# Another order at the passage from the weights' batches to the expert loop, two casts on POOL, and a place of weights read in six parts

## The chip, the cores and the metric

One NeuronCore of a Trainium2 chip runs the kernel. The metric is the device time of one execution in microseconds (us); the time before is the median of 3 runs. The profile is of one further execution.

Engines in the text: TensorE (PE; PEld is its weight load), VectorE (DVE), ScalarE (ACT), GpSimd (POOL) and SyncE (SP). SP issues most DMAs and ScalarE and POOL some. Each engine works through its own queue in order.

## The reference

One layer of a diffusion backbone over 512 tokens of width 1024: a mixer (pooling and retention, not touched here), then a feed-forward block of single-neuron experts with product keys, and a final RMSNorm. The part that matters:

```python
s = einsum('thpd,hpkd->thpk', q, keys)             # 8 heads, 2 halves, 128 keys each
s1, i1 = top_k(s[:, :, 0], 16); s2, i2 = top_k(s[:, :, 1], 16)
cand = s1[..., :, None] + s2[..., None, :]         # 16 x 16 candidates
cidx = i1[..., :, None] * 128 + i2[..., None, :]
best, pos = top_k(cand, 16); eidx = take_along_axis(cidx, pos)
g = softmax(best)
act = gelu(einsum('thkd,td->thk', u[eidx], hb))
out = einsum('thk,thkd->td', g * act, v[eidx])     # 16384 experts, u and v of width 1024
```

Each token uses 8 x 16 = 128 of the 16384 experts.

## The kernel before, in words

**Two ways to the same sum.** The 512 tokens are four blocks of 128. For block 0 the kernel gathers: for each of the 128 slots an indirect DMA on POOL's queue fetches, for each token, the row of u and v that its index names (`fetch`, L979); VectorE makes the dot product and adds the weighted row to `acc` (`dot`, `combine`, L987 and L998). For the three other blocks (384 tokens, side by side) it computes densely: the 16384 experts are taken as 128 planes of 128 experts. For a plane j, `up` multiplies its u (1024 x 128) with the tokens and applies GELU (ScalarE, L1106) into a tile `a`; the result is multiplied with a dense table G of weights, nearly all of it zeros (VectorE, L1141, "product" in the text), and `down` multiplies it with the plane's v and adds up in six PSUM banks Y.

**Three products for one.** A float32 matmul is made of three: each operand is split into `hi` (a cast, L163 for planes, L145 for `ph`) and `lo` (the difference, L168 for planes, L146 for `pl`), and `mm3` (L151 to L153) multiplies hi hi, then the two mixed ones. An `up` has 24 matmuls of 384 columns, done in two halves that a generator (`ups`, advanced by `run_up`) hands out; a `down` has 18 of 512 columns. `hi` of a plane is ScalarE's, `lo` VectorE's or POOL's.

**Loads.** Planes of u or v are 512 KB each and go by SP's queue into three buffers `raw` (L158); a load waits until `lo` has freed its buffer. `hi` and `lo` of planes have four buffers each.

**Weights.** The table G is built before the loop in 24 batches of 16 tokens (`onehots`, `weights`): one-hot matmuls into PSUM, a copy by ScalarE, a write to `gd` in HBM on ScalarE's DMA queue. The loop reads it back by places: a place has 8 planes for all tokens (1536 KB in rows of 512 bytes, as `gd` is laid out by batches), and there are 16 places and two buffers G. `place(p)` takes the buffer, `read(p, b0, b1)` issues a DMA for the batches b0 to b1 on SP's queue (L1120).

**The passage.** During the batches TensorE also runs the first `up` blocks ahead of the loop: AHEAD = 30 of them, 51 halves of 60 by the end of the batches. So 25 are complete then, number 25 is half done, and its successor 26 is split already. The order of all this part and of the loop is written out by hand (`manual_schedule`): each engine runs its instructions in program order. After the batches come, in this order: loads of v0 and v1; the last two reads of place 0; `place(1)` and its read; five times a half `up` and a `tick`; all remaining `up`s; the split of v0 (`lo` on POOL); three products; `weigh(0)`, which makes `ph` and `pl` of plane 0. `prep(n)` splits plane n of u and asks for the loads up to n + 3; within the generator it runs as the `up` before n begins.

**Ticks.** Top-k of block 0 is done head by head in five steps, each a stage of a generator (`topk`): step 1 on VectorE finds 16 of 128 in both halves, and two casts of the indices into `sf` follow (L927, L928, on ScalarE); step 2 adds up candidates on POOL (L936); step 3 on VectorE finds 16 of them; step 4 multiplies on POOL (L958); step 5 reduces on VectorE into `eidx`. `tick` (L1160) takes one new head and advances all that are under way by one step, oldest first; eight heads take 12 ticks.

**The loop.** Round j (0 to 127): read of a place in each round 8p + 6 (place p + 2), `weigh(j + 1)`, the split of v (`run_v`, up to plane j + 1; `lo` on POOL in the first 8 rounds), loads of u, `hi` of u, `down(j)`, the dot products and sums of the gathered slots with the products up to plane j + 3 between them, `lo` of u, an `up` in about four rounds of five, a `tick`. The gather begins in round GATHER = 8, with 1.2 slots a round; its buffers take the memory of block 0's top-k. In round 117 (LATE) three of its buffers are taken over for the end.

Of the kernel before, what the change touches and what calls it, by code (L numbers as in the profile page):

```python
# [20 lines left out]
P = 128  # L21
# [13 lines left out]
MG = 8  # L35
# [4 lines left out]
AHEAD = 30  # L40
JE = 121
LATE = 117
GATHER = 8
LAG = 2
CREDIT = 1.2
NT = 16
# [88 lines left out]
class Build:  # L135
# [765 lines left out]
    def topk(self, tp, h, s, blocks, bufs, eng=None):  # L901


        nc = self.nc
        NEG = -3.0e38
        n = len(blocks)
        b0 = blocks[0]
        tag = f"{n}"

        def new(shape, dt, name):  # L910
            return tp.tile([P, n] + shape, dt, name=name + tag, tag=name + tag, bufs=bufs)

        def best(of):

            for lo in (0, 8):
                for v, i, a in of:
                    nc.vector.max(out=v[:, lo:lo + 8], in_=a)
                for v, i, a in of:
                    nc.vector.max_index(i[:, lo:lo + 8], v[:, lo:lo + 8], a)
                if lo == 0:  # L920
                    for v, i, a in of:
                        nc.vector.match_replace(a, v[:, 0:8], a, NEG)

        sv, si = new([2, 16], F32, "sv"), new([2, 16], U32, "si")
        best([(sv[:, b, f], si[:, b, f], s[:, b, f]) for b in range(n) for f in range(2)])
        sf = new([2, 16], F32, "sf")
        nc.scalar.mul(sf[:, :, 0], si[:, :, 0], 128.0)  # L927
        nc.scalar.copy(sf[:, :, 1], si[:, :, 1])  # L928
        yield
        cs, ci = new([NCAND], F32, "cs"), new([NCAND], F32, "ci")  # L930
        for src, dst in ((sv, cs), (sf, ci)):
            o = 0
            for a0, m, w in CAND:
                A = src[:, :, 0, a0:a0 + m].unsqueeze(3).to_broadcast([P, n, m, w])
                B = src[:, :, 1, 0:w].unsqueeze(2).to_broadcast([P, n, m, w])
                nc.gpsimd.tensor_tensor(dst[:, :, o:o + m * w].rearrange("p h (a b) -> p h a b", a=m), A, B, ALU.add)  # L936
                o += m * w
            if b0:
                yield
        if not b0:  # L940
            yield
        bv, bi = new([16], F32, "bv"), new([16], U32, "bi")
        best([(bv[:, b], bi[:, b], cs[:, b]) for b in range(n)])

        pos = new([16, NI], F16, "pos")
        nc.vector.tensor_copy(pos, bi.unsqueeze(3).to_broadcast([P, n, 16, NI]))
        oh = tp.tile([P, n * 16, NC], F16, name="oh", tag="oh", bufs=1)
        sh = [P, n * 16, NC // NI, NI]
        nc.vector.tensor_tensor(oh.rearrange("p k (m i) -> p k m i", i=NI),
                                self.ioh[:, 0:NC].rearrange("p (m i) -> p m i", i=NI).unsqueeze(1).to_broadcast(sh),  # L950
                                pos.rearrange("p n k i -> p (n k) i").unsqueeze(2).to_broadcast(sh), ALU.is_equal)
        sl = slice(h * TOPK, (h + 1) * TOPK)
        nc.vector.tensor_tensor((self.gw if b0 else self.gw0)[:, :, sl], bv, bv[:, :, 0:1].to_broadcast([P, n, 16]), ALU.subtract)
        yield
        oe = tp.tile([P, n, 16, NCAND], F32, name="oe", tag="oe", bufs=1) if not b0 else \
            self.rt.tile([P, 2 * NB * P * NI], F32, name="oe", tag="ig", bufs=1)[:, :n * 16 * NCAND].rearrange(
                "p (n k c) -> p n k c", n=n, k=16)
        (nc.gpsimd if eng is None else eng).tensor_tensor(  # L958
            oe, oh.rearrange("p (n k) c -> p n k c", n=n)[:, :, :, :NCAND],
            ci.unsqueeze(2).to_broadcast([P, n, 16, NCAND]), ALU.mult)  # L960
        yield
        e = self.ef[:, :, sl] if b0 else new([16], F32, "e")
        nc.vector.tensor_reduce(e, oe, axis=AX.X, op=ALU.add)
        if not b0:
            nc.vector.tensor_copy(self.eidx[:, sl], e[:, 0])
# [143 lines left out]
    def experts(self):  # L1109
# [9 lines left out]
        def read(p, b0=0, b1=N // NT):  # L1119
            nc.sync.dma_start(Gs[p][:, b0:b1], self.gd[:, b0:b1, p * MG:(p + 1) * MG])  # L1120
# [4 lines left out]
        def run_v(to, eng):  # L1125

            while nv[0] < to:
                for n in range(nv[1], min(nv[0] + 2, P)):
                    vs[n] = load_v(n)
                    nv[1] += 1  # L1130
                vs[nv[0]] = self.split_w(vs[nv[0]], eng)
                nv[0] += 1
# [4 lines left out]
        def run_times(to):  # L1137
            while nt[0] < min(to, P):
                j = nt[0]
                a = acts[j].rearrange("p (b t) -> p b t", t=NT)  # L1140
                nc.vector.tensor_tensor(a, a, Gs[j // MG][:, :, j % MG], ALU.mult)  # L1141
                nt[0] += 1
# [17 lines left out]
        def tick(new=True):  # L1160

            if new:
                live.extend(islice(heads, 1))
            live[:] = [x for x in live if next(x, True) is None]
# [3 lines left out]
        with tc.tile_pool(name="hot", bufs=1) as hp:  # L1168
# [3 lines left out]
            for i, t0 in enumerate(todo):  # L1172
# [4 lines left out]
                if i in (13, 20):  # L1177
                    read(0, *{13: (0, 10), 20: (10, 18)}[i])
        self.rt_es.close()
        for n in range(2):  # L1180
            vs[n] = load_v(n)
        nv[1] = 2
        read(0, 18, 22)
        read(0, 22)
        self.dp = dp = self.pool("dense")
        place(1)
        read(1)
        for _ in range(5):
            self.run_up(1)
            tick()  # L1190
        self.run_up(2 * AHEAD)
        run_v(1, nc.gpsimd)
        self.pes.close()
        self.pp = es.enter_context(tc.tile_pool(name="pd", bufs=1, space=PSUM))
        self.ptags = {"ps": 2}
# [7 lines left out]

            return min(P, AHEAD + (j + 1) * (P - AHEAD) // JE)

        acts.update(enumerate(self.acts))
        run_times(3)
        ps[0] = weigh(0, nc.vector)

        f0 = None  # L1210

        for j in range(P):
            if j == GATHER:
                self.early.close()
                self.gp = es.enter_context(tc.tile_pool(name="gather", bufs=1, side="right"))
                self.acc = self.gp.tile([P, D], F32, name="acc", bufs=1)
            if j % MG == MG - 2 and j // MG + 2 < P // MG:
                place(j // MG + 2)
                read(j // MG + 2)
            deep = j >= JE  # L1220
            if j + 1 < P:
                ps[j + 1] = weigh(j + 1, nc.vector)
            run_v(min(P, j + 4 if deep else j + 2), nc.gpsimd if j < GATHER else nc.vector)
            while nl < goal(j + 2):
                us[nl] = self.load_u(nl)
                nl += 1
            hi = {}
            for n in range(ns, goal(j + 1)):
                hi[n] = self.split_hi(us[n])
            if j < P - 2:  # L1230
                for b in range(NB):
                    down(j, b, ps[j], vs[j])
                del ps[j], vs[j]

            ready = list(range(done, asked[0]))
            cr = [self.dot(s, slots[s]) for s in ready]
            run_times(j + 4)
            for s, act in zip(ready, cr):
                self.combine(s, slots.pop(s), act)
            done = asked[0]  # L1240
            for n in hi:
                us[n] = self.split_lo(us[n], hi[n], nc.vector)
                ns += 1
            while nu < goal(j):
                acts[nu] = self.up(nu, us.pop(nu))
                nu += 1
            tick()
            if j == GATHER - 1:
                self.softmax(self.gw0, self.z0)
            if j >= GATHER:  # L1250
                credit += CREDIT
                while credit >= 1 and fetched < S:
                    slots[fetched] = self.fetch(fetched)
                    fetched += 1
                    credit -= 1
            asked = asked[1:] + [fetched]
            if j == LATE:
                assert fetched == S
                fin = [self.gp.tile([P, 2 * D], F32, name="uv", tag="uv", bufs=NUV) for _ in range(3)]
                fin = [x[:, i * D:(i + 1) * D] for x in fin for i in range(2)]  # L1260
                self.row_bcast(fin[0], self.modc[:, 24:32])
                nc.sync.dma_start(fin[1], I["fg"].to_broadcast([P, D]))
            if LATE < j <= LATE + 4:
                b = j - LATE - 1
                nc.sync.dma_start(fin[2 + b], self.xd[b * P:(b + 1) * P])
            if j > LATE + 4 and done == S:
                if f0 is None:
                    f0 = self.finish(0, self.acc, [self.acc[:, 0:512], self.acc[:, 512:]], fin[2], fin[0], fin[1])
                    next(f0)
# [23 lines left out]
```

## Time and profile before

| | us |
|---|---|
| median of 3 runs | 1838.06 |
| the 3 runs | 1836.46, 1838.06, 1847.68 |
| the profiled execution | 1851.27 |
| its span, first to last instruction | 1849.3 |
| TensorE busy | 1751.0 (95%) |
| VectorE busy | 1346.7 (73%) |
| ScalarE busy | 776.6 (42%) |
| POOL busy | 435.6 (24%) |
| mean granted TensorE clock | 0.98 |

Times in rows are us from the start of the span. A row of the timeline has start, length, engine, line, operation, tiles, and in brackets how long the engine had been idle and what ended it. In rows of groups "x8" counts instructions. The granted clock is a share of 2.4 GHz; at 0.5 it is 1.2 GHz.

### The profile page before, as it was taken

Reading aid. Unit: us, or ns where it says so; the run is one execution under the profiler, and the core shown is the slowest. Engines: PE = TensorE matmul, PEld = TensorE weight load, DVE = VectorE, ACT = ScalarE, POOL = GpSimd, SP = SyncE. Lnnn points to the kernel's source line nnn. Section 1 sums busy time; section 2 is a strip of 40 time slices with the busy share of each in tenths; the row PEclk is TensorE's granted clock in tenths of the full one; section 3 lists DMA queues with packets and bytes.
Section 4 is the critical chain, followed back from the end, with each engine's and each line's share of the span. In section 5 each row is a group of like instructions: output and inputs, shape, how many; then the busy total and the mean of one; then the engine's idle time right before and its main releaser. Section 6 shows DMA issues by size and latency. Waiting matters only on the chain.

```text
span 1849.3 us, 25951 instructions
## 1 busy us (share of the span) xinstructions
PE 1751.0 (95%) x9913; PEld 1566.5 (85%) x9913; DVE 1346.7 (73%) x2402; ACT 776.6 (42%) x1320; POOL 435.6 (24%) x387
## 2 busy tenths in 40 slices
PE   7999999999999988877999999999999999999996
PEld 4889988888989988876898889999978898888885
DVE  6865365663569999987767688787768787767756
ACT  6343344223334358852434344443434443434333
POOL 2222220001148710024522222222212222222100
PEclk9999999999999999998999999999999999999998
DMA  7211134774142227772497798898878888887752
GB/s 304 103 47 46 58 131 131 237 243 145 63 142 92 81 101 263 277 237 89 156 374 290 274 329 309 327 331 295 328 282 303 317 308 298 333 302 266 267 170 91
DMA packets 132428, 404.00 MB, mean 218 GB/s; under 512 B 9680, under 2 KB 59088, under 8 KB 112720
## 3 DMA queue, kind: packets, MB, share of 16 engines
q1 hardware_dynamic: 109984, 241.38, 38.8%
q0 software_dynamic: 18432, 134.23, 18.4%
q10 hardware_dynamic: 3888, 26.74, 3.5%
q8 instruction: 77, 1.26, 0.3%
q14 instruction: 47, 0.39, 0.1%
HBM read 372.95 MB, written 29.36 MB: 218 GB/s over the span
## 4 chain that ended last, share of the span: by engine, by line
PE 38%; DVE 9%; DMA 8%; ACT 4%; issue 3%; POOL 1%; ACTq 0%; DVEq 0%; POOLq 0%
DMA raw<-uvd 8%; PE Y L152 7%; PE Y L153 7%; PE Y L151 7%; PE ps L153 6%; PE ps L151 6%; PE ps L152 6%; DVE lo L168 2%; DVE o L1071 2%; ACT st L1084 2%; ACT hi L163 2%; DVE eq L1068 1%; DVE uv L987 1%; DMA gd<-st 1%; DVE o L1069 0%
## 5 line engine op out<-in xcount | busy, mean ns | idle before, releaser
L168 DVE TENSOR_TENSOR lo<-raw,hi 128x1024 fp32r<-128x1024 f32 x285 | 358.6, 1259 | 139.8 <-ACT hi L163 138.4
L163 ACT CAST hi<-raw 128x1024 fp32r<-128x1024 f32 x332 | 344.0, 1050 | 267.8 <-DMA raw<-uvd 186.3
L153 PE MATMUL ps<-hfT,lo 128*128 128x384 f32 x1120 | 380.4, 340 | 17.8 <-DVE lo L168 17.8
L151 PE MATMUL ps<-hfT,hi 128*128 128x384 f32 x1120 | 382.1, 341 | 11.1 <-ACT hi L163 11.1
L152 PE MATMUL ps<-hfT,hi 128*128 128x384 f32 x1120 | 378.3, 338 | 0.1
L979 POOL DMA_INDIRECT uv<-uv,eidx x128 | 196.5, 1535 | 623.7 <-DVE acc L998 599.2
L151 PE MATMUL Y<-hi,ph 128*128 128x512 f32 x768 | 305.4, 398 | 16.5 <-ACT hi L163 12.8
L152 PE MATMUL Y<-lo,ph 128*128 128x512 f32 x768 | 307.6, 401 | 9.6 <-POOL lo L168 7.0
L153 PE MATMUL Y<-hi,pl 128*128 128x512 f32 x768 | 306.5, 399 | 0.5 <-DVE pl L146 0.5
L153 PEld LDWEIGHTS ps<-hfT,lo 128*128 128x128 f32 x1120 | 212.4, 190 | 23.9 <-DVE lo L168 23.8
L151 PEld LDWEIGHTS ps<-hfT,hi 128*128 128x128 f32 x1120 | 212.8, 190 | 16.5 <-ACT hi L163 12.3
L152 PEld LDWEIGHTS ps<-hfT,hi 128*128 128x128 f32 x1120 | 212.8, 190 | 4.4 <-POOL hfT L146 0.5
L151 PEld LDWEIGHTS Y<-hi,ph 128*128 128x128 f32 x768 | 147.7, 192 | 48.1 <-ACT hi L163 14.7
L998 DVE SCALAR_TENSOR_TENSOR acc<-uv,act,acc 128x1024 f32<-128x1024 f32 x127 | 163.1, 1284 | 33.1 <-ACT act L990 22.3
L152 PEld LDWEIGHTS Y<-lo,ph 128*128 128x128 f32 x768 | 147.4, 192 | 42.9 <-POOL lo L168 8.9
L153 PEld LDWEIGHTS Y<-hi,pl 128*128 128x128 f32 x768 | 147.6, 192 | 32.5 <-DVE pl L146 1.4
L168 POOL TENSOR_TENSOR lo<-raw,hi 128x1024 fp32r<-128x1024 f32 x47 | 117.8, 2515 | 204.5 <-ACT hi L163 204.5
L146 DVE TENSOR_TENSOR pl<-a,ph 128x384 fp32r<-128x384 f32 x128 | 75.0, 586 | 118.5 <-ACT ph L145 118.5
L1106 ACT ACTIVATE a<-ps 128x384 f32<-128x384 f32 x128 | 62.7, 490 | 227.7 <-PE ps L153 221.3
L987 DVE SCALAR_TENSOR_TENSOR uv<-uv,hf 128x1024 f32<-128x1024 f32 x128 | 154.5, 1220 | 0.0
L1084 ACT ACTIVATE st<-ps 128x512 f32<-128x512 f32 x96 | 90.9, 1111 | 13.4 <-DMA gd<-st 7.2
L989 ACT ACTIVATE act<-act 128x1 f32<-128x1 f32 x128 | 25.9, 202 | 162.4 <-DVE uv L987 162.2
(285 smaller groups left out, 2913.5 us busy)
## 6 DMA issues: line engine op xcount, KB each, us to landing
raw<-uvd SPq DMA_DIRECT2D x252, 512.0 KB, 5.8
ada<-ada SPq DMA_DIRECT2D x48, 512.0 KB, 4.9
gd<-st ACTq DMA_DIRECT2D x24, 1024.0 KB, 5.4
G<-gd SPq DMA_DIRECT2D x15, 1536.0 KB, 14.3
raw<-w_in SPq DMA_DIRECT2D x44, 512.0 KB, 4.3
raw<-wq SPq DMA_DIRECT2D x16, 512.0 KB, 3.8
raw<-ret_out SPq DMA_DIRECT2D x8, 512.0 KB, 4.7
raw<-w_out SPq DMA_DIRECT2D x8, 512.0 KB, 3.7
```

What stands on the lines that cost most here:

```text
L146: (eng_lo or nc.vector).tensor_tensor(lo, src, hi.bitcast(F32), ALU.subtract)
L151: mm(out, a[0], b[0], start=first, stop=False)
L152: mm(out, a[0], b[1], start=False, stop=False)
L153: mm(out, a[1], b[0], start=False, stop=last)
L163: self.nc.scalar.copy(hi, raw)
L168: eng.tensor_tensor(lo, raw, hi.bitcast(F32), ALU.subtract)
L979: self.nc.gpsimd.indirect_dma_start(out=t, out_offset=None, in_=self.I["uv"], in_offset=bass.IndirectOffsetOnAxis(ap=self.eidx[:, s:s + 1] ...
L987: nc.vector.scalar_tensor_tensor(t[:, :D], t[:, :D], 1.0, self.hf, ALU.mult, ALU.mult, accum_out=act[:, 0:1])
L998: nc.vector.scalar_tensor_tensor(self.acc, t[:, D:], act[:, 1:2], self.acc, ALU.mult, ALU.add)
L1071: nc.vector.tensor_tensor(wide(o2[:, r]), wide(eq), tokens(self.gq[:, r]), ALU.mult)
L1084: nc.scalar.mul(st[:, :, t:t + 4].rearrange("p m t -> p t m"), ps, 1.0 / GSCALE)
L1106: nc.scalar.activation(a, ps[:, :N], AF.Gelu)
```

## The change

Block 0's top-k casts go to POOL (the two other lines are for the other blocks, unchanged). After the batches the two last reads of place 0 come first, then the loads of v0 and v1 and place 1 with its read. Then planes 27 and 28 of u are split, two ticks, three halves of `up`, the split of plane 29, a tick, two halves, the split of v0, a tick, three products and `weigh(0)`, the remaining four halves, a tick. In the loop a tick is left out in every fourth round, the gather begins in round 9, and place p + 2 is read in six parts of four batches (256 KB) in the rounds 8p + 5 to 8p + 10, behind that round's loads.

```diff
-GATHER = 8
+GATHER = 9
@@ topk
-        nc.scalar.mul(sf[:, :, 0], si[:, :, 0], 128.0)
-        nc.scalar.copy(sf[:, :, 1], si[:, :, 1])
+        if b0:
+            nc.scalar.mul(sf[:, :, 0], si[:, :, 0], 128.0)
+            nc.scalar.copy(sf[:, :, 1], si[:, :, 1])
+        else:
+            nc.gpsimd.tensor_scalar(sf[:, :, 0], si[:, :, 0], 128.0, None, ALU.mult)
+            nc.gpsimd.tensor_copy(sf[:, :, 1], si[:, :, 1])
@@ experts, after the batches
         self.rt_es.close()
+        read(0, 18, 22)
+        read(0, 22)
         for n in range(2):
             vs[n] = load_v(n)
         nv[1] = 2
-        read(0, 18, 22)
-        read(0, 22)
         self.dp = dp = self.pool("dense")
         place(1)
         read(1)
-        for _ in range(5):
-            self.run_up(1)
-            tick()
+        k = len(self.acts)
+        self.prep(k + 2, nc.vector)
+        self.prep(k + 3, nc.vector)
+        tick()
+        tick()
+        self.run_up(3)
+        self.prep(k + 4, nc.vector)
+        tick()
+        self.run_up(2)
+        run_v(1, nc.gpsimd)
+        tick()
+        acts.update(enumerate(self.acts))
+        run_times(3)
+        ps[0] = weigh(0, nc.vector)
         self.run_up(2 * AHEAD)
-        run_v(1, nc.gpsimd)
+        acts.update(enumerate(self.acts[1:], 1))
+        tick()
         self.pes.close()
...
-        acts.update(enumerate(self.acts))
-        run_times(3)
-        ps[0] = weigh(0, nc.vector)
@@ experts, in the loop
-            if j % MG == MG - 2 and j // MG + 2 < P // MG:
-                place(j // MG + 2)
-                read(j // MG + 2)
             deep = j >= JE
             if j + 1 < P:
                 ps[j + 1] = weigh(j + 1, nc.vector)
-            run_v(min(P, j + 4 if deep else j + 2), nc.gpsimd if j < GATHER else nc.vector)
+            run_v(min(P, j + 4 if deep else j + 2), nc.gpsimd if j + 1 < GATHER else nc.vector)
             while nl < goal(j + 2):
                 us[nl] = self.load_u(nl)
                 nl += 1
+
+            p, k = divmod(j - MG + 3, MG)
+            if p >= 0 and p + 2 < P // MG and k < 6:
+                if k == 0:
+                    place(p + 2)
+                read(p + 2, 4 * k, 4 * k + 4)
...
-            tick()
+            if j % 4 < 3:
+                tick()
```

## Rows read from the trace of the kernel before

**Rows 1.** Stretches: length, busy us of PE, PEld, DVE, ACT, POOL; clock, DMA share, GB/s.

```profile
805.50:844.00 38.50, 25.37 (x113) 22.94 (x111) 25.71 (x123) 12.43 (x26) 11.08 (x43) 0.82 0.47 156
844.00:907.20 63.20, 55.24 (x245) 46.45 (x246) 55.32 (x136) 18.37 (x30) 39.27 (x54) 0.95 0.38 121
...
976.00:990.00 14.00, 12.17 (x53) 10.80 (x52) 11.98 (x14) 5.26 (x10) 4.92 (x3) 0.88 0.71 253
...
1039.00:1051.00 12.00, 8.32 (x28) 6.25 (x27) 7.94 (x11) 5.36 (x8) 1.68 (x1) 0.72 0.50 173
1051.00:1340.00 289.00, 289.00 (x1446) 260.85 (x1445) 231.19 (x287) 120.12 (x231) 73.39 (x47) 1.00 0.87 319
1340.00:1358.00 18.00, 13.46 (x48) 10.47 (x47) 9.45 (x13) 6.37 (x11) 1.67 (x1) 0.81 0.73 243
...
1532.00:1546.00 14.00, 11.67 (x50) 9.81 (x50) 7.70 (x9) 4.31 (x7) 1.68 (x1) 0.88 0.65 240
...
1660.00:1675.00 15.00, 10.69 (x38) 8.55 (x38) 8.55 (x12) 4.81 (x9) 1.68 (x1) 0.77 0.57 194
...
1050.06:1058.32 8.26, 8.26 (x43) 7.56 (x42) 6.24 (x8) 2.34 (x5) 1.67 (x1) 1.00 0.97 336
```

**Rows 2.** Timeline of TensorE in the passage.

```profile
834.57 0.69 PE L151 MATMUL ps<-hfT,hi 128*128 128x384 f32 x1 [5.98 <-ACT hi L163]
...
844.00 0.50 PE L151 MATMUL Y<-hi,ph 128*128 128x512 f32 x1 [1.92 <-ACT ph L145]
```

**Rows 3.** Timeline of ScalarE in the passage.

```profile
833.19 0.22 ACT L927 ACTIVATE sf<-si 128x16 f32<-128x16 uint32 x1 [5.33 <-DVE si L919]
...
833.48 1.04 ACT L163 CAST hi<-raw 128x1024 fp32r<-128x1024 f32 x1
```

**Rows 4.** Tile raw: the load issued at 1026.4, behind G's read of 1022.6.

```profile
DMA to landing us min/median/max: 15.4/15.4/15.4
```

**Rows 5.** DMA issues of the page: count, KB each, median us to landing.

```profile
raw<-uvd SPq DMA_DIRECT2D x252, 512.0 KB, 5.8
...
G<-gd SPq DMA_DIRECT2D x15, 1536.0 KB, 14.3
...
G<-gd SPq DMA_DIRECT2D x1, 128.0 KB, 4.5
```

**Rows 6.** Tile G, 1051 to 1325: its four reads.

```profile
L1120 SPq DMA_DIRECT2D G<-gd x4: 530/561/649, 1084.8 to 1267.1; - x4
...
DMA to landing us min/median/max: 11.4/14.1/14.6
```

**Rows 7.** Tile G: the read of place 1, issued at 814.8.

```profile
DMA to landing us min/median/max: 9.4/9.4/9.4
```

**Rows 8.** Groups of POOL by form, 844 to 907: busy us, mean ns.

```profile
L168 POOL TENSOR_TENSOR lo<-raw,hi 128x1024 fp32r<-128x1024 f32 x8 | 19.6, 2451 | 20.3 <-ACT hi L163 20.3
...
L936 POOL TENSOR_TENSOR cs<-sv 128x10 f32<-128x10 f32 x4 | 2.4, 588 | 0.0
...
L936 POOL TENSOR_TENSOR ci<-sf 128x16 f32<-128x16 f32 x4 | 0.8, 207 | 0.0
```

**Rows 9.** Timeline of SP's DMA issues in the passage.

```profile
813.60 1.86 SPq L1120 DMA_DIRECT2D G<-gd x3
```

**Rows 10.** Timeline of VectorE in the passage and in the first rounds.

```profile
812.99 0.48 DVE L917 MAX8 sv<-s 128x8 f32<-128x128 f32 x2
...
817.62 0.29 DVE L917 MAX8 sv<-s 128x8 f32<-128x128 f32 x1
...
827.14 1.04 DVE L963 TENSOR_REDUCE e<-oe 128x16 f32<-128x864 f32 x1
828.22 0.17 DVE L965 CAST eidx<-e 128x16 int32<-128x16 f32 x1
...
861.09 2.53 DVE L168 TENSOR_TENSOR lo<-raw,hi 128x1024 fp32r<-128x1024 f32 x1 [0.87 <-ACT hi L163]
```

**Rows 11.** Groups of VectorE by form, 1051 to 1340: the products.

```profile
L1141 DVE TENSOR_TENSOR a<-a,G 128x384 f32<-128x384 f32 x39 | 21.6, 554 | 0.0
```

## The prediction, made before the changed kernel was run

> **What bounds the kernel now.** I read the page's busy shares first, then the table of stretches, because the shares average over stages. From about 850 us on, TensorE is the bound wherever nothing goes wrong: in the stretch 1051 to 1340 it is busy 289.0 of 289.0 us with 1446 matmuls, 0.20 us each, at full granted clock, with the DMA engines at 0.87 [rows 1]. One `up` block (24 matmuls) and one round of `down` (18) take 8.26 us together [rows 1]; they are of about equal length, so I use 4.2 us for an `up`, 2.1 us for half of one, and 4.1 us for a `down`. Time can only be won where TensorE falls short of this pace, and the table shows three such places; in each I take the length of the stretch less its matmuls at 0.20 us [rows 1].
>
> (a) The passage, 805.5 to 844.0: nine halves of `up` remain (the second half of number 25, then 26 to 29), 9 x 2.1 = 18.9 us of work in 38.5 us. Lost: 19.6 us. (b) The first rounds, 844.0 to 907.2: 245 matmuls, 49.0 us of work in 63.2. Lost: 14.2 us. (c) Four short stretches later, granted clock 0.72 to 0.88 where 1.00 is 2.4 GHz: 976 to 990 loses 14.0 - 53 x 0.2 = 3.4, 1039 to 1051 loses 6.4, 1340 to 1358 loses 8.4, 1532 to 1546 loses 4.0, 1660 to 1675 loses 7.4. These five sum to 29.6 us (the first, too, is at a reduced clock).
>
> Next, who ends each loss. In the passage TensorE waits 5.98 us at 834.57 for ScalarE's `hi` of a u plane, and 1.92 us at 844.00 for ScalarE's `ph` [rows 2]. ScalarE itself could not start that `hi` before 833.48, as two `sf` casts stand ahead of it in its queue, and these waited 5.33 us for VectorE's top-k step [rows 3]. In the late stretches the cause is the whole-place read of G: a weight load issued at 1026.4, behind the read issued at 1022.6, landed after 15.4 us [rows 4], against 5.8 us at the median [rows 5]. So SP's loads land in the order of their issue, and 1536 KB (14.3 us at the median [rows 5]) go first. Not every whole read hurts: four with landings of 11.4 to 14.6 us lie in the stretch that loses nothing [rows 1, 6]. The loss is a coincidence of a read with bursts of gathers, hence it differs from execution to execution.
>
> **The change, part by part.**
>
> *A place in six parts.* Each of 14 places is read by six DMAs of 256 KB, in rounds 8p+5 to 8p+10, instead of one of 1536 KB in round 8p+6. Bytes and 512-byte rows are the same. The first part stands in SP's queue where the whole read stood: behind the loads of round 8p+5 and ahead of those of 8p+6; so it waits for the same release of the buffer (the products of round 8p+4). The last is issued in round 8p+10, is first used by the products of round 8p+13, and has three rounds, over 22 us, to land. What a load behind it waits for: place 1 landed 9.4 us after its issue, a 128 KB read 4.5 us [rows 5, 7], so (9.4 - 4.5) us for 1408 KB, 3.5 us per MB: a part holds the queue for 0.9 us where nothing else runs, and for a sixth of 14.3, 2.4 us, in the loop. Loads then land after about 5.8 + 2.4 = 8.2 us. Loads delayed by up to the 11.4 to 14.6 us of the four harmless reads cost nothing, so 8.2 is well inside. I expect the five stretches to lose 4 us in place of 29.6: -26 us. The bounds: none of it goes (0), if the bursts of gathers alone are the cause; all of it goes (-30). Seventy more issues of about half a microsecond are SP's, which is no bound.
>
> The Trainium skill ("DMA: Bandwidth & Descriptors", section "Measured (HBM→SBUF, 128 partitions, SWDGE, issued from GpSimd)") speaks against this: batch DMAs to at least 1 MiB, as each has a fixed cost; its formula, made for the gather's path, gives 2.0 us plus bytes / 436 GB/s, by which I estimate six parts at 15.6 us and the whole at 5.6 us. By it a place would cost 10 us more. The trace has the three reads of the passage issued within 1.86 us, and the first ones landed while the last was still moving, so the fixed part overlaps here.
>
> *Casts of the gathered places on POOL.* Sixteen casts of 128x16 leave ScalarE. They are short; what counts is where they wait: each pair waits for the end of VectorE's newest top-k step. ScalarE no longer stops there, so `ph` and `hi` go ahead; instead POOL stops, and behind the casts in its queue stands `lo` of the next v plane, 2.45 us [rows 8]. The trace has no such cast on POOL; the nearest row is POOL's add of 128x16, 0.21 us, the farthest a small add at 0.59 us [rows 8]; I take 0.2 each, 0.4 to 1.2 the pair. Could it be nothing or a gain by itself? Yes, as POOL's adds on `sf` no longer wait for another engine; I count no gain.
>
> *The passage.* The two last reads of place 0 move ahead of the loads of v0 and v1. They wait for the last write of `gd`; the three reads of before go out from 813.60 on within 1.86 us [rows 9], so SP is held until about 814.4, v0 goes out then (7 us later than now, hidden: v0 is needed after 829), then v1, place 1, and u29. Before, place 1 landed at 814.8 + 9.4 = 824.2 [rows 7]; with 512 KB more ahead of it (1.8 us by the rate above) at 826, and u29 behind it at about 828.
>
> `hi` and `lo` of 27 and 28 now come ahead of all top-k steps, so TensorE runs 25b to 28b without a stop, to about 821 (805.5 + 7 x 2.1, and 0.5 at 27). Then it waits for u29: `hi` at 829, `lo` at 830.3; seven or eight us idle, then 29 partly at a lowered clock (the stretch has 0.82 now [rows 1]). This is the same stop as now, five us earlier. But VectorE's queue has `lo` of 29 ahead of the third tick. A step 1 and a step 3 of top-k take 817.62 - 812.99 = 4.6 us, a step 5 with its cast 1.2 [rows 10]. So the third tick ends at 835, the fourth at 839.6, the first product (0.55 us [rows 11]) at 840.2, `ph` at 840.7, and with two GELUs behind it the first `down` starts at about 842, against 844.0. I take -2 us; +4 if place 1 lands later, -9 if u29 is not held up. The fifth tick (5.8 us) is then still to be done, in round 0, where before it was over.
>
> *First rounds, ticks in three of four, gather a round later.* VectorE per ticked round: tick 5.8, product 0.55, `pl` about as much, `lo` of a u plane up to 2.53 (with POOL running [rows 10]): 9.4 us, against TensorE's 8.3: it is 1.1 us late. Before, ScalarE's stops stood on top of that. Round 1 is late by more: the fifth tick ends at 842.6 + 5.8 = 848.4, the casts at 848.8, `lo` of v1 at 851.3, and `down` of round 0 was through at 846.1: 5.2 us. Three more ticked rounds at 1.1 give 3.3, the lowered clock about 1. Lost: 9.5 in place of 14.2, so -5 (bounds +6, -10). The round without a tick lets VectorE catch up, by when the heavy ticks are over. The gather starts one round later: 107 rounds from round 9 end at 115, still ahead of round 117, where its slots are taken over; 0.
>
> Sum: -26 - 2 - 5 = -33, and I round to -32: 1851.3 - 32 = 1819 in the terms of the profiled execution. That one is 13.2 us above the median of the three runs, which spread over 11.2 us. If all the 13.2 were stalls of kind (c), the median after would be the same 1819, as the stalls are gone in both; if none, 1838 - 32 = 1806. I take a value between, nearer to the first: **1815 us**.
>
> **The rivals.** *Stalls in the timed runs are few* (and the passage gives nothing): 13 of the 29.6 us of stalls are already missing at the median, 17 are left, 13 of those go: 1838 - 13 = 1825. For: the spread of the runs. Against: the fastest run, 1836.5, is hardly below the median. *The parts cost as much as the whole*: each of the six holds the queue for its own landing, 4.5 us, not 0.9. The loads then land 4.5 us later in six rounds of eight, and a burst of gathers makes that long enough; (c) stays, 1838 - 7 = 1831. Against: the overlapping reads of the passage. The batching rule of the Trainium skill ("DMA: Bandwidth & Descriptors", the section named above) would come to this here. *Slower*: POOL and VectorE become the bound of the passage. Place: `lo` of 29 ahead of two ticks on VectorE, and `lo` of v behind the casts on POOL. It decides from the point where u29 lands after about 833, for instance if place 1 takes the loop's 14.3 us: then the first `down` starts at 847 (+3), and the four ticked rounds each wait for a `lo` of v that POOL ends some 3 us late (casts at 0.6, `lo` slowed by VectorE) rather than 1.1, +8; with (c) rare in the timed runs, 1838 + 3 + 8 = 1849. Against: nothing else is on the queue in the passage.
>
> **How the numbers follow.** Forecast 0.58 (its own range 1804 to 1824), few stalls 0.27, parts as costly 0.08, slower 0.07. The range 1801 to 1834 holds the first two and most of the third. About 1% (18 us) is what a measurement of this kernel tells from no change: faster by that means below 1819.7, which the forecast reaches in most of its range: 0.60. Slower by that needs over 1856, the far end of the last rival: 0.04. The rest, 0.36, is the same.
>
> **What would show it.** Right: no weight load in the loop lands later than about 11 us, no stretch after 907 with a granted clock under 0.95, ScalarE's waits for top-k gone and POOL's in their place; TensorE's one long stop in the passage before number 29, from 821 to 829, and the first `down` near 842. Wrong: a weight load of 15 us after a 256 KB read; `lo` of v on POOL ending the waits of each of the first rounds by 3 us or more; a first `down` after 846.

## The result, and the profile after

The changed kernel takes 1818.67 us (median of 4 runs, 1814.78 to 1821.25) against 1837.99 (4 runs, 1836.46 to 1847.68): ratio 0.9881, 95% interval 0.9855 to 0.9907 (the two medians alone give 0.9895). That is faster by a little over 1%, with 1815 forecast and 1801 to 1834 as the range. The profiled execution took 1820.35 us with a span of 1818.6, against 1851.27 and 1849.3.

First the table of stretches of the changed kernel (columns as in [rows 1]): the passage, the first rounds, and the rest of the loop up to 1775, which is cut so that the two stretches that lose time stand by themselves.

```profile
806.10:843.60 37.50, 21.45 (x113) 20.13 (x110) 21.29 (x95) 10.58 (x16) 11.32 (x40) 0.85 0.53 178
843.60:904.90 61.30, 55.46 (x246) 47.41 (x247) 57.26 (x163) 17.66 (x24) 42.54 (x71) 0.92 0.31 102
904.90:948.00 43.10, 43.10 (x215) 38.68 (x214) 24.56 (x30) 16.99 (x25) 13.38 (x9) 1.00 0.77 279
948.00:965.00 17.00, 14.45 (x65) 12.81 (x64) 11.13 (x14) 6.82 (x13) 3.35 (x2) 0.90 0.73 271
965.00:1150.00 185.00, 180.47 (x895) 161.32 (x894) 144.21 (x179) 75.68 (x145) 44.31 (x29) 1.00 0.85 309
1150.00:1775.00 625.00, 625.00 (x3131) 564.42 (x3130) 489.37 (x603) 261.56 (x493) 140.67 (x91) 1.00 0.85 310
```

With 0.20 us a matmul, as for [rows 1], the passage loses 37.5 - 18.9 = 18.6 us (before 19.6), the first rounds 61.3 - 246 x 0.2 = 12.1 (before 14.2), the stretch 948 to 965 loses 17.0 - 65 x 0.2 = 4.0, and the next one 185.0 - 895 x 0.2 = 6.0. From 1150 to 1775 TensorE does not stop once: 625.0 of 625.0 us. The five stretches that lost 29.6 us have become one that loses 4.0, which is 25.6 us less. Of the 6.0 us, 4.5 are four equal stops of 1.13 us, 38.7 us apart, each ended by `lo` of u on VectorE; the kernel before has such stops too, three of them behind the last of its five stretches (first row the changed kernel, second the one before).

```profile
1027.41 0.44 PE L153 MATMUL ps<-hfT,lo 128*128 128x384 f32 x1 [1.13 <-DVE lo L168]
```
```profile
1688.22 0.44 PE L153 MATMUL ps<-hfT,lo 128*128 128x384 f32 x1 [1.14 <-DVE lo L168]
```

A count that does not depend on how the stretches are chosen takes equal work: the same 4056 matmuls from the end of the first rounds on (first row before, second row after).

```profile
907.21:1755.40 848.19, 827.37 (x4056) 740.53 (x4056) 637.45 (x791) 342.66 (x644) 198.95 (x129) 0.98 0.83 305
```
```profile
904.88:1727.55 822.67, 815.59 (x4056) 734.23 (x4056) 640.83 (x790) 342.46 (x642) 201.71 (x130) 1.00 0.87 316
```

By it the loop gives 25.5 of the 30.7 us by which the span fell. The first rounds give two and the first `down` comes 0.4 us earlier; the remaining three lie after these matmuls.

TensorE's timeline, the places of [rows 2]:

```profile
828.84 0.69 PE L151 MATMUL ps<-hfT,hi 128*128 128x384 f32 x1 [7.16 <-ACT a L1110]
```
```profile
843.59 0.79 PE L151 MATMUL Y<-hi,ph 128*128 128x512 f32 x1 [8.42 <-ACT a L1110]
```

The profile puts both waits down to a GELU, the last instruction of ScalarE before; ScalarE's own timeline (compare [rows 3]) shows what ScalarE waited for:

```profile
827.35 1.04 ACT L163 CAST hi<-raw 128x1024 fp32r<-128x1024 f32 x1 [13.94 <-DMA raw<-uvd]
...
842.25 0.51 ACT L145 CAST ph<-a 128x384 fp32r<-128x384 f32 x1 [12.53 <-DVE a L1145]
```

The first is the load of u29, which stands last among the transfers that SP issues in the passage. The second is VectorE, which had two ticks between `lo` of 29 and the first product. So TensorE stops for 7.2 and 8.4 us where before it stopped for 4.1 (the row below, of the kernel before), 6.0 and 1.9, and the first `down` starts at 843.6, against 844.0.

```profile
821.29 0.69 PE L151 MATMUL ps<-hfT,hi 128*128 128x384 f32 x1 [4.08 <-ACT hi L163]
```

The DMA issues of the page (compare [rows 5]): the median load of a plane lands after 6.0 us in place of 5.8, a part after 7.6 us.

```profile
raw<-uvd SPq DMA_DIRECT2D x252, 512.0 KB, 6.0
...
G<-gd SPq DMA_DIRECT2D x85, 256.0 KB, 7.6
```

The casts, by tile `sf`, 806 to 905, and two of the waits of that stretch (us in total, times, longest us):

```profile
L931 POOL TENSOR_SCALAR sf<-si x8: 252/253/258, 816.3 to 880.8; 128x16 f32<-128x16 uint32 x8
L932 POOL CAST sf<-si x8: 196/442/448, 816.5 to 881.0; 128x16 f32<-128x16 uint32 x8
```
```profile
POOL sf L931 <- DVE si L919: 180.3, 8, 161.3
...
PE Y L152 <- POOL lo L168: 5.8, 4, 1.9
```

ScalarE's waits for top-k are gone, POOL's stand in their place (161.3 of the 180.3 us are idleness before the first cast), and `lo` of v behind them ends four waits of TensorE, 5.8 us in all and 1.9 at the longest. Before it ended five, 7.0 us in all and 1.9 at the longest, so POOL's new wait costs TensorE nothing more there.

### The profile page after: what moved, and what is told of

The parts are those of the page before. It is cut to its first block, busy times and chain, and to the rows that moved or that the text cites. A ratio compares the mean times of both kernels' runs of the same rounds, so it can differ in the third digit from the quotient of the medians.

```text
span 1818.6 us, 26049 instructions
## 1 busy us (share of the span) xinstructions
PE 1733.3 (95%) x9913; PEld 1556.5 (86%) x9913; DVE 1348.6 (74%) x2402; ACT 774.6 (43%) x1304; POOL 442.8 (24%) x403
## 3 DMA queue, kind: packets, MB, share of 16 engines
q8 instruction: 77, 1.26, 0.3%
## 4 chain that ended last, share of the span: by engine, by line
PE 46%; DVE 7%; ACT 5%; DMA 3%; issue 2%; POOL 1%; ACTq 0%; DVEq 0%; POOLq 0%
PE Y L152 8%; PE Y L153 8%; PE Y L151 8%; PE ps L153 7%; PE ps L151 7%; PE ps L152 7%; ACT st L1088 3%; DMA raw<-uvd 2%; DVE lo L168 1%; DVE o L1075 1%; ACT hi L163 1%; DMA gd<-st 1%; DVE eq L1072 1%; DVE uv L991 1%; POOL lo L168 0%
## 5 line engine op out<-in xcount | busy, mean ns | idle before, releaser
L168 DVE TENSOR_TENSOR lo<-raw,hi 128x1024 fp32r<-128x1024 f32 x285 | 364.1, 1279 | 102.7 <-ACT hi L163 100.9
L153 PE MATMUL ps<-hfT,lo 128*128 128x384 f32 x1120 | 378.5, 338 | 16.9 <-DVE lo L168 16.9
L151 PE MATMUL Y<-hi,ph 128*128 128x512 f32 x768 | 301.0, 392 | 10.1 <-ACT a L1110 8.4
L152 PE MATMUL Y<-lo,ph 128*128 128x512 f32 x768 | 302.9, 394 | 6.4 <-POOL lo L168 5.8
L153 PE MATMUL Y<-hi,pl 128*128 128x512 f32 x768 | 302.6, 394 | 0.0
L153 PEld LDWEIGHTS Y<-hi,pl 128*128 128x128 f32 x768 | 145.1, 189 | 30.7 <-DVE pl L146 0.3
L1088 ACT ACTIVATE st<-ps 128x512 f32<-128x512 f32 x96 | 91.0, 1109 | 13.2 <-DMA gd<-st 7.1
```

The lines of the kernel that those rows point to most:

```text
L151: mm(out, a[0], b[0], start=first, stop=False)
L152: mm(out, a[0], b[1], start=False, stop=False)
L153: mm(out, a[1], b[0], start=False, stop=last)
L168: eng.tensor_tensor(lo, raw, hi.bitcast(F32), ALU.subtract)
L1088: nc.scalar.mul(st[:, :, t:t + 4].rearrange("p m t -> p t m"), ps, 1.0 / GSCALE)
```

## The experiments

Each ran beside the kernel before on the same chip; times are medians, ratios are to that kernel. "By theory A" means that the time came out as that theory of the expectation had it.

**The parts alone.** The diff of the loop's read, put into the kernel before, nothing else.

> The kernel before with nothing but the reading in six parts over six rounds. Theory A (the gain is the whole read of G that stood ahead of plane loads in SP's queue): nearly all of the gain, about 1822 us, and in the profile no stretch after 907 us with a plane load landing after 15 us except at the gather's start. Theory B (the gain is the passage and ScalarE freed of the casts): 1833 to 1837 us. The passage's end, the first down, stays at 844 us by both.

1820.77 us, ratio 0.9897 (0.9878 to 0.9916). By theory A. The passage and first rounds are as before (rows below, compare [rows 1]), its first `down` at 843.4; after 907 no stop over 1.2 us is left up to 1770 but one of 1.6 us at the gather's start.

```profile
804.60:843.40 38.80, 25.97 (x114) 23.55 (x110) 25.73 (x123) 12.42 (x26) 11.10 (x43) 0.78 0.47 154
843.40:906.60 63.20, 55.78 (x246) 47.16 (x247) 55.39 (x136) 18.38 (x30) 39.28 (x54) 0.92 0.33 105
```

**All but the parts.**

```diff
+            if j % MG == MG - 2 and j // MG + 2 < P // MG:
+                place(j // MG + 2)
+                read(j // MG + 2)
...
-            p, k = divmod(j - MG + 3, MG)
-            if p >= 0 and p + 2 < P // MG and k < 6:
-                if k == 0:
-                    place(p + 2)
-                read(p + 2, 4 * k, 4 * k + 4)
```

> The changed kernel with a place read whole again, in round 8p + 6. Theory A: 1833 to 1836 us, the passage and first rounds 3 us shorter than before, and two to five stops of TensorE of 3 to 8 us each, some 20 us after a read's issue. Theory B: 1818 to 1823 us.

1833.57 us, ratio 0.9962 (0.9939 to 0.9985). By theory A again: 0.4% for all the rest of the change, 1.0% for the parts. The two ratios multiplied give 0.986, inside the interval of the whole. From 907 to 1770 TensorE stops for 16.0 us in all (rows below), against 7.1 in the changed kernel and 6.9 with the parts alone; the stops are back, though shorter than expected, with 3.1 us as the longest.

```profile
PE ps L153 <- DVE lo L168: 9.6, 8, 2.0
PE Y L151 <- ACT hi L163: 3.7, 2, 3.1
PE Y L152 <- DVE lo L168: 2.7, 5, 0.8
```

The spread of the runs says the same: the 12 runs of this kernel spread over 18.8 us and the 17 of the kernel before beside them over 16.9, the 6 of the parts alone over 5.2. What the whole read costs differs from execution to execution.

**Six parts at once.**

```diff
-            p, k = divmod(j - MG + 3, MG)
-            if p >= 0 and p + 2 < P // MG and k < 6:
-                if k == 0:
-                    place(p + 2)
-                read(p + 2, 4 * k, 4 * k + 4)
+            if j % MG == MG - 3 and j // MG + 2 < P // MG:
+                place(j // MG + 2)
+                for k in range(6):
+                    read(j // MG + 2, 4 * k, 4 * k + 4)
```

> The changed kernel with the six reads of 256 KB all issued in round 8p + 5, behind its loads, where the first part stands now. Theory A (what counts is how much of G stands ahead of a plane load at a time): as bad as whole, 1832 to 1836 us, plane loads of 14 us and more behind the six. Rival C (what counts is the size of one DMA, in parts they mix with the gather's packets): 1817 to 1821 us, no such loads.

1824.04 us, ratio 0.9916 (0.9891 to 0.994): neither. It is better than the whole read by some 9 us and worse than the parts over six rounds by some 5. On average over the 14 places the last of the six landed 13.9 us after the first one's issue, the whole read 13.8 after its own; the next plane load landed 15.9 and 16.3 us after that issue. So the burst is as long, and a place cut up but not spread still delays the loads. What differs is SP: with several DMAs under way one issue takes up to 5.5 us (tile G, durations min/median/max in ns), so plane loads go out later, and count as less late by the time from their own issue.

```profile
L1124 SPq DMA_DIRECT2D G<-gd x84: 426/696/5487, 893.6 to 1693.6; - x84
```

Why 0.4 us less is worth 9 us is not settled. That stops begin only from some lateness on, so that small differences decide, would fit, but no run here tests it.

**The whole read on ScalarE's DMA queue**, otherwise as in "all but the parts".

```diff
-                read(j // MG + 2)
+                p = j // MG + 2
+                nc.scalar.dma_start(Gs[p], self.gd[:, :, p * MG:(p + 1) * MG])
```

> The changed kernel with a place read whole, in round 8p + 6, but issued on ScalarE's DMA queue. Theory A (plane loads are late because they land behind G in SP's queue): plane loads of more than 12 us become rare (5 or fewer after 907 us in place of 13), 1817 to 1823 us. Rival G (the DMA engines are simply full while 1536 KB and the gather's bursts move, whatever the queue): 1831 to 1836 us, loads as late as with the whole read on SP's queue.

1822.42 us, ratio 0.9904 (0.9876 to 0.9932). By theory A in time; by the count of late loads half of it, 7 over 12 us in place of 13. The tiles show the turn: G now lands last (first fence, ScalarE's queue), and no plane load takes over 14.6 us (second, tile raw from 905 on; with the whole read on SP's queue 17.0, in the kernel before 20.4).

```profile
L1233 ACTq DMA_DIRECT2D G<-gd x14: 525/526/600, 892.3 to 1690.8; - x14
...
DMA to landing us min/median/max: 8.6/18.7/26.5
```
```profile
DMA to landing us min/median/max: 3.6/6.5/14.6
```

A place may take 26.5 us, as it has time; what costs is a plane load behind it in the same queue. So 11 of the 15 us between the whole read on SP's queue (1833.6) and the parts (1818.7) come without cutting anything. Rival G, for which the queue makes no difference, falls with that; that late loads became half as many, and not rare, leaves the full DMA engines a share in them.

**Three parts.**

```diff
-            if p >= 0 and p + 2 < P // MG and k < 6:
+            if p >= 0 and p + 2 < P // MG and k < 3:
...
-                read(p + 2, 4 * k, 4 * k + 4)
+                read(p + 2, 8 * k, 8 * k + 8)
```

> The changed kernel with a place in three parts of 512 KB over three rounds. Theory A (the amount of G ahead of a plane load at a time): 512 KB, a third of the whole, is still well inside what the loads' lead covers; 1817 to 1822 us. If the stops grow in proportion to the part's size, two sixths of the way from 1818.7 to 1833.6 at the least: 1823 to 1826 us.

1814.27 us, ratio 0.9864 (0.9836 to 0.9892): no worse than six. It would be too much to call it better, since the intervals overlap and, below, three and six agree. One difference is plain in the profiles, though, and explains the one larger stop that the changed kernel kept. Its parts go out in the rounds 8p + 5 to 8p + 10, so the sixth part of the first place read in the loop falls into the burst with which the gather begins in round 9 (six slots issued from 925.8 to 933.0). Issued at 933.7, it landed after 14.4 us, and the two loads behind it after 14.4 and 17.3 (first fence); the `hi` of the later one began at 954.15, and TensorE's stop of 1.96 us ended at 958.13. The three parts end in round 8p + 7, before the burst; the same two loads landed after 10.0 and 11.8 us (second fence), and TensorE did not stop there (third). All six kernels of this study whose six parts reach into that burst had a load of 16.4 to 18.0 us at this place.

```profile
L158 SPq DMA_DIRECT2D raw<-uvd x2: 328/328/328, 934.9 to 936.9; - x2
...
DMA to landing us min/median/max: 14.4/15.8/17.3
```
```profile
L158 SPq DMA_DIRECT2D raw<-uvd x2: 327/328/328, 934.3 to 936.2; - x2
...
DMA to landing us min/median/max: 10.0/10.9/11.8
```
```profile
903.00:963.00 60.00, 60.00 (x302) 54.09 (x301) 39.68 (x51) 24.91 (x39) 16.72 (x11) 1.00 0.81 295
```

**The casts on ScalarE again.** Only the diff of `topk` undone.

> The changed kernel with the casts of block 0 on ScalarE again. Theory A: in the ticked rounds ph and hi of the planes wait again for the end of VectorE's step, two to four us in each of four rounds; 1822 to 1827 us. Rival D (POOL's wait has only taken the place of ScalarE's, as lo of v stands behind it): 1817 to 1820 us.

1825.19 us, ratio 0.9923 (0.9904 to 0.9942); some 6 us slower than the changed kernel. By theory A: POOL's wait is the cheaper one. Two waits of it, 806 to 905, are ScalarE's for top-k, which is back, and VectorE's for the `hi` behind it:

```profile
ACT sf L927 <- DVE si L919: 48.5, 8, 8.5
DVE lo L168 <- ACT hi L163: 21.4, 8, 9.6
```

**Parts and casts, with the old passage.** The kernel before with those two edits; the old order, a tick in every round, the gather from round 8.

> The kernel before with the six parts and with the casts on POOL, but the old order of the passage, a tick in every round and the gather from round 8. If the casts are the part of the passage that helps: 1812 to 1817 us, below the changed kernel, as TensorE's two stops before 28 and 29 shrink without u29 standing in VectorE's way. If the new order is needed for it: 1819 to 1822 us, like the parts alone (1820.8).

1815.12 us, ratio 0.9871 (0.9844 to 0.9899): as fast as the whole change, without the new order of the passage. The passage loses 36.5 - 18.9 = 17.6 us, the first rounds 60.2 - 246 x 0.2 = 11.0, together 28.6, against 30.7 in the changed kernel:

```profile
806.20:842.70 36.50, 24.11 (x113) 22.46 (x110) 26.01 (x123) 11.09 (x16) 15.75 (x53) 0.86 0.51 166
842.70:902.90 60.20, 53.81 (x246) 45.88 (x247) 57.28 (x136) 17.65 (x24) 42.14 (x60) 0.94 0.34 110
```

Four kernels now read a place in six parts and differ in the order of the passage (with the ticks and the gather's start) and in the engine of the casts:

| us | casts on ScalarE | casts on POOL |
|---|---|---|
| old order | 1820.8 | 1815.1 |
| new order | 1825.2 | 1818.7 |

The casts on POOL are worth about 6 us in both rows, and in neither do the single runs of the two kernels overlap. The new order wins nothing in either column; by the medians it is slower by about 4, which the overlapping intervals do not settle. What the expectation gave as the reason was not it: the two stops before 28 and 29 did not shrink (3.75 and 5.92 us, against 4.08 and 5.98), they only end by VectorE's `lo` now. Against the parts alone the passage is 2.3 us shorter (36.5, 38.8) and the first rounds 3.0 (60.2, 63.2); which of the smaller waits makes this up was not followed.

**u29 first.** One line in the changed kernel.

```diff
         self.rt_es.close()
+        self.ask(AHEAD)
         read(0, 18, 22)
```

> The changed kernel with the load of u29 issued ahead of all of the passage's other loads and reads. Theory E (the passage's gain went lost as u29 stands behind place 1 in SP's queue, and two ticks, the first product and ph behind the lo of 29): u29 lands before 813 in place of 827.3, TensorE runs 25b to 29b without a long stop, the first down starts at 831 to 834 in place of 843.6, and the time is 1807 to 1811 us. Rival F (VectorE's top-k work bounds the way to the first rounds anyway, what is won at the first down is lost in rounds 0 to 3): 1815 to 1819 us.

1807.55 us, ratio 0.983 (0.9803 to 0.9857). By theory E. Load of u29 (tile raw, issued at 808.2) and the first `down`:

```profile
L158 SPq DMA_DIRECT2D raw<-uvd x1: 327/327/327, 808.2 to 808.2; - x1
...
DMA to landing us min/median/max: 4.3/4.3/4.3
```
```profile
834.30 0.79 PE L151 MATMUL Y<-hi,ph 128*128 128x512 f32 x1 [8.01 <-ACT a L1110]
```

TensorE's stop before number 29 is gone, the first `down` comes 9.3 us earlier, 0.3 later than expected. The stop before it is about as long as it was, 8.0 us against 8.4: its end is VectorE's two ticks.

**The products first, and where the ticks go.** On top of "u29 first":

```diff
         self.prep(k + 4, nc.vector)
-        tick()
-        self.run_up(2)
         run_v(1, nc.gpsimd)
-        tick()
         acts.update(enumerate(self.acts))
         run_times(3)
         ps[0] = weigh(0, nc.vector)
+        self.run_up(2)
+        tick()
         self.run_up(2 * AHEAD)
         acts.update(enumerate(self.acts[1:], 1))
-        tick()
```

with GATHER = 11 and CREDIT = 1.25, as three ticks in place of five remain in the passage; and once with all five ticks there, the last three behind the products (GATHER 9, CREDIT 1.2).

> The kernel with u29 first, and: the split of v0, the three products and ph, pl of plane 0 ahead of the third tick; three ticks in the passage, the other nine in the loop's rounds 0, 1, 2, 4, 5, 6, 8, 9, 10; the gather from round 11 with 1.25 slots a round. Theory H (what is left of the loss is VectorE's queue: two ticks of 4.6 us ahead of the first product, and one of 5.8 ahead of pl and lo of plane 1): first down at 826 to 828, no stop over 2 us in rounds 0 to 3, 1792 to 1798 us. Rival F (VectorE's top-k work as a whole bounds the first rounds): what is won at the first down is lost in rounds 1 to 8, 1803 to 1808 us.

> The kernel with u29 first, the split of v0, the three products and plane 0's ph and pl ahead of the third tick, but all five ticks still in the passage and the gather from round 9. Theory H: the first down starts at 826 to 829, but the second waits for lo of v1 on POOL, behind the casts of the fifth tick, until about 841 to 844; no more than 2 us gained on the kernel with u29 first, 1805 to 1809 us. If the place of the products alone were the loss: 1797 to 1801 us.

Three ticks: 1797.82 us, ratio 0.978 (0.9751 to 0.9809). Five: 1807.83, ratio 0.9839 (0.9807 to 0.9871). By theory H in both. With five the first `down` starts early too, at 826.5, but TensorE then stands before the second, 11.7 us at the longest (its waits, 804 to 880; first fence): the products first, by themselves, are worth nothing (1807.83 against 1807.55). With three the passage takes 21.65 us for 18.9 us of work, the first rounds lose 60.65 - 255 x 0.2 = 9.7 (second fence); TensorE's longest stop there is 1.8 us (third fence), within the 2 us that H allowed, and the first `down` came at 824.65, before the 826 to 828 of H. Two ticks fewer with the products in their old place were not run, and the three-tick kernel has the later gather besides, so the 10 us belong to these edits together.

```profile
PE Y L152 <- POOL lo L168: 14.9, 3, 11.7
```
```profile
803.00:824.65 21.65, 19.62 (x114) 18.66 (x110) 16.04 (x57) 10.48 (x16) 7.71 (x25) 1.00 0.83 278
824.65:885.30 60.65, 53.44 (x255) 45.94 (x256) 57.03 (x175) 19.51 (x27) 43.56 (x74) 1.00 0.34 110
```
```profile
PE Y L152 <- POOL lo L168: 7.2, 6, 1.8
```

The kernel with three ticks is the fastest of the study, 2.2% below the kernel before. The same with three parts:

> The same with a place in three parts of 512 KB over three rounds. If part size between 256 and 512 KB does not matter: within 2 us of the former. If the smaller burst counts: 3 to 6 us slower.

1798.92 us, ratio 0.9788 (0.9759 to 0.9816): within 2 us, as expected if 256 or 512 KB are the same. Here the gather begins in round 11, so the sixth part is out before its burst, and neither kernel has a stop at the gather's start.

## Why the prediction came out as it did

**The parts: right in mechanism, and in size for the profiled executions.** Forecast -26 in the terms of the profiled execution, measured -25.6 by stretches and -25.5 by equal work (the other edits' effect on the loop included). That execution was 13 us above the median, and in the medians the parts are worth less: 19 us alone (1840.2 to 1820.8), 15 on top of the rest (1833.6 to 1818.7). The reason given, a whole place ahead of plane loads in SP's queue, is borne out by the parts alone (most of the gain without the rest), by all but the parts (stops come back), and by ScalarE's queue (most of the gain without any cutting). Two things said to show it right did not hold: loads of over 11 us do occur, eight of them, and the stretch 948 to 965 has a granted clock of 0.90, under 0.95. And one thing said to show it wrong did happen once: a load of 17.3 us behind a part of 256 KB, at the gather's start, and from it the stop that remained. There a part delayed the loads behind it by 4.4 and 5.5 us (against the kernel with three parts), not by the 2.4 of the working; that its 4.0 us equal the 4 that were left over in the forecast is chance, as no stop was named. Everywhere after 965 no load landed later than 13.1 us, and TensorE had no stop over 1.2 us there up to 1770. The rival by which six parts would cost as much as the whole falls with the parts alone: 1820.8, not 1831. The batching rule of the Trainium skill ("DMA: Bandwidth & Descriptors", section "Measured (HBM→SBUF, 128 partitions, SWDGE, issued from GpSimd)") asks for 1 MiB and more in a DMA; the formula that the prediction quotes with it stands on the same page in the section "Anatomy of one DMA — SWDGE (gpsimd) path". The runs do not bear the rule out for this place: parts of 256 KB and 512 KB do equally well (1797.8 and 1798.9 us), and the read of 1536 KB on SP's queue is the slow one (1833.6 against 1818.7 us).

**The profiled execution against the median: chosen on the wrong side.** The two ends given were 1819 (the 13.2 us above the median are stops) and 1806 (none are); 1815 was taken between them, and 1818.67 is the first end. Profile and median after lie 1.7 us apart, where they lay 13 apart before: with the stops the difference went, as the smaller spread of the runs with parts says too. That the median came within 4 us of the forecast owes something to this choice and to terms that went wrong in both directions below.

**The passage: the order of events right, the gain half or less.** Forecast -2, measured -1.0 by the loss and -0.4 by the first `down`. TensorE ran 25b to 28b with no stop but one of 0.5 us, u29 landed at 827.3 (828 forecast) as last of its queue, the stop ended at 828.8 (829), the first `down` began at 843.6 (842). Behind the missing 1.6 us is a wait that the working did not have: step 3 of the second head stood behind POOL, which had `lo` of v0 ahead of step 4 of the first, while both need the one buffer `oh` (VectorE's timeline, first row: a cast that takes 0.20 us elsewhere took 1.26 and ended with POOL's `lo`; second: the wait).

```profile
835.66 1.26 DVE L950 CAST pos<-bi 128x64 f16<-128x64 uint32 x1
...
838.70 0.63 DVE L953 TENSOR_TENSOR oh<-ioh,pos 128x896 f16<-128x896 f16 x1 [1.78 <-POOL oe L962]
```

That so little would come of the passage was in the working: u29 behind place 1, and two ticks ahead of the first product. The first was then undone for 11 us; the second, together with two ticks fewer in the passage, for another 10.

**The first rounds: -2.1 in place of -5.** The term that was mis-sized is "the lowered clock about 1". Behind the stop of 8.4 us the first `down` ran for some 6 us, and the second for some 3.5 behind its own wait of 1.9, at 1.2 GHz; 23 matmuls started 0.43 us apart in place of 0.23, so the term measured 4.6 us (first fence, two matmuls of the first `down`, at the low and at the full clock; then the stretch of the changed kernel with two `down`s and an `up`, and the one of the same 60 matmuls before; granted clock third from the end):

```profile
844.61 0.63 PE L153 MATMUL Y<-hi,pl 128*128 128x512 f32 x1
...
850.22 0.39 PE L152 MATMUL Y<-lo,ph 128*128 128x512 f32 x1
```

```profile
843.60:862.60 19.00, 17.09 (x60) 14.03 (x61) 18.38 (x65) 4.74 (x6) 13.64 (x28) 0.75 0.16 56
```
```profile
844.00:859.96 15.96, 14.44 (x60) 12.03 (x60) 13.34 (x35) 3.96 (x7) 8.48 (x13) 0.89 0.30 99
```

19.0 us for 60 matmuls, against 15.96: three us more than before, 2.7 of them in TensorE's busy time, though `ph` and `hi` came in time. Part of this stands in for another term: while the first `down` ran slowly, POOL and VectorE caught up, so that the second waited 1.9 us for `lo` of v1 and not the 5.2 of the working, and the waits for POOL's `lo` come to 5.5 us in these rounds (1.9, 1.8, 1.8) in place of 5.2 + 3.3. POOL's terms were a little low too: a pair of casts takes 0.7 us in place of 0.4, `lo` of v 2.69 in place of 2.45 (groups of POOL by form, 843 to 905):

```profile
L168 POOL TENSOR_TENSOR lo<-raw,hi 128x1024 fp32r<-128x1024 f32 x7 | 18.8, 2694 | 1.2 <-ACT hi L163 1.2
```

The gain that the casts do bring, 6 us by undoing them, was counted only as ScalarE's part of the first rounds; without the new order it is as large (1820.8 to 1815.1 us). So the -7 that the working gave to the passage and the first rounds together were -3.1 in the profiled executions, and behind them stand 6 us from the casts and a new order that won nothing. The rival "slower" did not come: u29 landed before 833, the point named for it.

## What to carry to other kernels

A large transfer that has time should not stand in one queue ahead of small ones that have none: cut it and spread it, or give it another queue. Cutting it finer than needed brought nothing here, and a part that falls into a burst of other transfers delayed the loads behind it all the same, so their place matters as well as their size. In a passage written out by hand, look for the one load or step that the first instruction of the next stage needs, and see what stands ahead of it in each queue that it passes: here one load moved to the front was worth 11 us, and three short products moved ahead of two long ticks another 10, but only with two of the five ticks taken out of the passage; a reordering without these was worth nothing. An idle stretch of the matrix engine can cost more than its length: behind the stops of 8.4 and 1.9 us the matmuls at the lower clock took 4.6 us more.

## What the runs showed of the hardware beyond what was expected

The second cast of a pair on POOL took 0.20 us at the least and 0.44 us at the median, the five long ones all beside VectorE's products or `pl`, the three short ones not; a cast of VectorE went from 0.20 to 1.26 us beside POOL's `lo`. The Trainium skill ("GPSIMD Engine Reference", section "1. Specifications") says that POOL shares its SBUF interfaces with VectorE; these numbers agree, and in proportion they are larger for short instructions than for the long `lo` of POOL, which took 2.35 us for v0 and 2.69 in the mean of the first rounds.

Six DMAs in a row from SP are not issued at the pace of one: 0.43 us at the least, 0.70 at the median, 5.5 at the most, while the loads behind them wait to be issued by SP.

SP's DMAs landed in the order of their issue throughout: of the 326 from 806 us on in the changed kernel, and of the 256 with the whole read, none landed before one that was issued earlier.
